# RMSNorm with SiLU on one core: VectorE's product moved ahead of the next block's sums in three blocks, and one more square given to VectorE in five

## Chip, cores, metric

One core of one Trainium2 chip, nothing else running on it. The metric is the device time of the kernel in microseconds (us), each figure the median of several runs. A profile of one execution goes with each kernel; its span is some 2 us shorter than the time, since a little of the time lies outside it.

## What is computed

The input x is 8 x 1024 rows of 2048 float32 values. Each row is divided by its root mean square, multiplied by gamma, and put through SiLU.

```python
def reference(x, gamma, eps):
    rms = np.sqrt(np.mean(x ** 2, axis=-1, keepdims=True) + eps)
    out = gamma * x / rms
    return (out * (1 / (1 + np.exp(-out)))).astype(np.float32)
```

## The kernel before

The rows are cut into 16 blocks of 4 MB: 128 partitions with four rows (J = 4) each. Six block buffers are kept (BUFS = 6). Loads are issued on ScalarE's queue, stores on SyncE's. In each block the sums of squares of two rows are taken by ScalarE and of two by VectorE; ScalarE takes the root, VectorE the inverse and the product with gamma, and ScalarE SiLU in place, on half a block at a time.

```python
    def sums(b, after_first=()):
        ss = small.tile([P, J], f32, name="ss")
        na = J // 2
        for j in range(na, J):
            nc.vector.tensor_tensor_reduce(out=junk_v, in0=row(b, j), in1=row(b, j), ...,
                                           accum_out=ss[:, j:j + 1])
        for j in range(na):
            nc.scalar.activation(out=junk_a, in_=row(b, j), func=ACT.Square,
                                 accum_out=ss[:, j:j + 1])
            if j == 0:
                for s in after_first:
                    load(s)
        ...                                   # root of the mean, on ScalarE

    def finish(b, halves=False):
        for j in range(J):
            nc.vector.scalar_tensor_tensor(out=row(b, j), in0=row(b, j), scalar=rstds[b][:, j:j + 1],
                                           in1=g, op0=ALU.mult, op1=ALU.mult)
            if j % 2:
                cols = slice((j - 1) * d, (j + 1) * d)
                nc.scalar.activation(out=blocks[b][:, cols], in_=blocks[b][:, cols], func=ACT.Silu)
                if halves:
                    nc.sync.dma_start(out=ob[b][:, cols], in_=blocks[b][:, cols])
    ...
        sums(0); invert(0); finish(0); store(0); sums(1); invert(1)     # six lines in the kernel
        for b in range(1, last - 1):
            sums(b + 1, after_first=[b + 3] if BUFS <= b + 3 < nblk else [])
            finish(b)
            store(b)
            invert(b + 1)
        finish(last - 1); store(last - 1)
        sums(last); invert(last); finish(last, halves=True)
```

## Time and profile before

| | before |
|---|---|
| time, median of 3 runs | 317.25 us (317.17 to 317.58) |
| span of the profile | 315.1 us |
| VectorE busy | 223.6 us, 71% |
| ScalarE busy | 223.7 us, 71% |
| bytes moved | 134.24 MB, mean 426 GB/s |
| DMA row of the slices | 9 in 38 of 40 slices |

How to read it: the page cuts the span into forty slices and gives the busy share of each in tenths (9 is 90% or more). DVE is VectorE, ACT is ScalarE, q10 the queue of the loads, q1 that of the stores. A busy share says how much an engine works, not whether the end waits for it: here two engines are at 71% and the sixteen DMA engines at 99%. The lines themselves stand in the prediction below.

### The profile page before, as it was taken

Reading aid. Unit: us, or ns where it says so; the run is one execution under the profiler, and the core shown is the slowest. Engines: PE = TensorE matmul, PEld = TensorE weight load, DVE = VectorE, ACT = ScalarE, POOL = GpSimd, SP = SyncE. Lnnn points to the kernel's source line nnn. Section 1 sums busy time; section 2 is a strip of 40 time slices with the busy share of each in tenths; the row PEclk is TensorE's granted clock in tenths of the full one; section 3 lists DMA queues with packets and bytes.
Section 4 is the critical chain, followed back from the end, with each engine's and each line's share of the span. In section 5 each row is a group of like instructions: output and inputs, shape, how many; then the busy total and the mean of one; then the engine's idle time right before and its main releaser. Section 6 shows DMA issues by size and latency. Waiting matters only on the chain.

```text
span 315.1 us, 438 instructions
## 1 busy us (share of the span) xinstructions
PE 2.1 (1%) x8; PEld 0.5 (0%) x8; DVE 223.6 (71%) x147; ACT 223.7 (71%) x144; POOL 0.2 (0%) x4
## 2 busy tenths in 40 slices
PE   0200000000000000000000000000000000000000
PEld 0000000000000000000000000000000000000000
DVE  0679499999295692957939488493984929994920
ACT  1357958999768677686676776766867668779550
POOL 0000000000000000000000000000000000000000
DMA  8999999999999999999999999999999999999997
GB/s 334 408 458 408 391 458 408 458 408 458 408 459 408 459 408 453 412 458 412 453 412 453 420 445 424 445 420 445 428 437 428 441 433 433 441 424 441 424 418 314
DMA packets 4762, 134.24 MB, mean 426 GB/s; under 512 B 532, under 2 KB 532, under 8 KB 536
## 3 DMA queue, kind: packets, MB, share of 16 engines
q10 hardware_dynamic: 2304, 67.11, 49.8%
q1 hardware_dynamic: 2456, 67.12, 49.4%
q14 instruction: 2, 0.02, 0.0%
HBM read 67.12 MB, written 67.11 MB: 426 GB/s over the span
## 4 chain that ended last, share of the span: by engine, by line
DMA 65%; DVE 18%; ACT 10%; issue 2%; DVEq 1%; ACTq 0%
DMA xt<-in_x_dram 65%; DVE xt L87 13%; ACT xt L91 6%; DVE junk_v L67 4%; ACT junk_a L71 2%; ACT L77 2%; DVEq L161 1%; ACT L91 0%; ACT rms L77 0%; DVE rstd L82 0%; DVE ss L67 0%; DVEq L67 0%; ACTq L77 0%
## 5 line engine op out<-in xcount | busy, mean ns | idle before, releaser
L87 DVE SCALAR_TENSOR_TENSOR xt<-xt,rstd,g 128x2048 f32<-128x2048 f32 x64 | 146.2, 2347 | 0.1
L91 ACT ACTIVATE xt<-xt 128x4096 f32<-128x4096 f32 x32 | 115.5, 3616 | 39.2 <-DVE xt L87 39.2
L67 DVE CUSTOM_DVE_ANT_0 junk_v<-xt 128x2048 f32<-128x2048 f32 x32 | 73.6, 2299 | 56.6 <-DMA xt<-in_x_dram 55.9
L71 ACT ACTIVATE junk_a<-xt 128x2048 f32<-128x2048 f32 x32 | 60.1, 1879 | 26.7 <-DMA xt<-in_x_dram 26.2
L77 ACT ACT_TABLE_LOAD x15 | 19.2, 1283 | 9.9 <-DVE ss L67 9.9
L91 ACT ACT_TABLE_LOAD x15 | 19.2, 1283 | 0.3
L82 DVE RECIPROCAL rstd<-rms 128x4 f32<-128x4 f32 x16 | 2.8, 173 | 10.8 <-ACT rms L77 10.8
L111 DVE COPY g<-junk_v 128x2048 f32<-128x2048 f32 x1 | 2.3, 2292 | 9.3 <-PE junk_v L109 9.3
L71 ACT ACTIVATION_READ_ACCUMULATOR junk_a<-xt 128x1 f32 x32 | 6.0, 186 | 0.0
L77 ACT ACTIVATE rms<-ss,eps_t 128x4 f32<-128x4 f32 x16 | 4.8, 297 | 1.3 <-DVE ss L67 1.1
L67 DVE DVE_READ_ACCUMULATOR2_ANT ss<- 128x1 f32 x32 | 4.5, 141 | 0.0
L104 ACT ACT_TABLE_LOAD x1 | 1.3, 1283 | 3.8 <-issue 3.8
L109 PE MATMUL junk_v<-grow,ones 1*128 1x512 f32 x8 | 2.1, 1132 | 8.1 <-DMA grow<-in_gamma_dram 8.1
L102 DVE MEMSET ones<- 128x128 f32 x1 | 0.2, 165 | 0.8 <-PEq L147 0.8
L109 PEld LDWEIGHTS junk_v<-grow,ones 1*128 1x128 f32 x8 | 0.5, 306 | 8.1 <-issue 8.1
L104 ACT ACTIVATE junk_a<-ones 128x1 f32<-128x1 f32 x1 | 0.2, 175 | 0.0
L147 POOL MEMSET const-bfloat16-1.0<- 128x1 bf16 x1 | 0.1, 101 | 0.0
L147 POOL MEMSET const-uint8-127<- 128x1 uint8 x1 | 0.1, 101 | 0.0
L147 POOL MEMSET const-float32-0.0<- 128x1 f32 x1 | 0.1, 98 | 0.2 <-issue 0.2
L147 POOL MEMSET const-float32-1.0<- 128x1 f32 x1 | 0.1, 98 | 0.0
L103 DVE MEMSET eps_t<- 128x1 f32 x1 | 0.1, 59 | 0.0
## 6 DMA issues: line engine op xcount, KB each, us to landing
xt<-in_x_dram ACTq DMA_DIRECT2D x16, 4096.0 KB, 38.7
out_dram<-xt SPq DMA_DIRECT2D x15, 4096.0 KB, 34.6
out_dram<-xt SPq DMA_DIRECT2D x2, 2048.0 KB, 9.0
grow<-in_gamma_dram SPq DMA_DIRECT2D x1, 8.0 KB
```

The source lines that it names most:

```text
L67: nc.vector.tensor_tensor_reduce(out=junk_v, in0=row(b, j), in1=row(b, j), scale=1.0, scalar=0.0, op0=ALU.mult, op1=ALU.add, accum_out=ss[ ...
L71: nc.scalar.activation(out=junk_a, in_=row(b, j), func=ACT.Square, accum_out=ss[:, j:j + 1])
L77: nc.scalar.activation(out=rms, in_=ss, func=ACT.Sqrt, scale=1.0 / d, bias=eps_t)
L82: nc.vector.reciprocal(out=rstd, in_=rmss.pop(b))
L87: nc.vector.scalar_tensor_tensor(out=row(b, j), in0=row(b, j), scalar=rstds[b][:, j:j + 1], in1=g, op0=ALU.mult, op1=ALU.mult)
L91: nc.scalar.activation(out=blocks[b][:, cols], in_=blocks[b][:, cols], func=ACT.Silu)
L102: nc.vector.memset(ones, 1.0)
L104: nc.scalar.activation(out=junk_a[:, 0:1], in_=ones[:, 0:1], func=ACT.Square)
L109: nc.tensor.matmul(junk_v[:, c * w:(c + 1) * w], ones[k:k + 1, :], grow[k:k + 1, :], start=True, stop=True)
L111: nc.vector.tensor_copy(out=g, in_=junk_v)
L147: nc = _bacc.Bacc("TRN2", target_bir_lowering=False, num_devices=1)
L161: with _tile.TileContext(nc) as tc:
```

## The change

Its intent: in the first three blocks the product, and with it the store, should not wait behind the next block's sums on VectorE; in the middle, ScalarE should be relieved of a square in every other block. The two functions `sums` and `finish` are split so that their parts can be put in any order. Cut to the core:

```diff
+    def share(b):
+        return 1 if 4 <= b <= 12 and b % 2 == 0 else 2      # rows whose squares ScalarE takes
...
-        for b in range(1, last - 1):
-            sums(b + 1, after_first=[b + 3] if BUFS <= b + 3 < nblk else [])
-            finish(b)
-            store(b)
-            invert(b + 1)
+        for b in range(last):
+            loads = [b + 3] if BUFS <= b + 3 < nblk else []
+            if b < SOON:                                    # SOON = 3
+                multiply(b)
+                squares_scalar(b + 1, loads)
+                silu(b)                                     # stores the block at its end
+                squares_vector(b + 1)
+                root(b + 1)
+            elif b < last - 1:
+                squares_scalar(b + 1, loads)
+                squares_vector(b + 1)
+                root(b + 1)
+                multiply(b)
+                silu(b)
+            else:
+                multiply(b)
+                silu(b)
+                ...                                         # squares and root of the last block
+            invert(b + 1)
```

More of the change, by code (lines that the diff above doesn't have):

```diff
@@ L50 @@
     junk_v = psum.tile([P, d], f32, name="junk_v")
-    blocks, rmss, rstds = {}, {}, {}
+    blocks, sss, rmss, rstds = {}, {}, {}, {}
     def load(b):
@@ L59, in row, with squares_scalar, squares_vector, root @@
         return blocks[b][:, j * d:(j + 1) * d]
-    def sums(b, after_first=()):
-        ss = small.tile([P, J], f32, name="ss")
-        na = J // 2
-        for j in range(na, J):
+    def squares_scalar(b, loads=()):
+        sss[b] = small.tile([P, J], f32, name="ss")
+        for j in range(share(b)):
+            nc.scalar.activation(out=junk_a, in_=row(b, j), func=ACT.Square,
+                                 accum_out=sss[b][:, j:j + 1])
+            if j == 0:
+                for s in loads:
+                    load(s)
+    def squares_vector(b):
+        for j in range(share(b), J):
             nc.vector.tensor_tensor_reduce(
                 out=junk_v, in0=row(b, j), in1=row(b, j), scale=1.0, scalar=0.0,
-                op0=ALU.mult, op1=ALU.add, accum_out=ss[:, j:j + 1])
-        for j in range(na):
-            nc.scalar.activation(out=junk_a, in_=row(b, j), func=ACT.Square,
-                                 accum_out=ss[:, j:j + 1])
-            if j == 0:
-                for s in after_first:
-                    load(s)
+                op0=ALU.mult, op1=ALU.add, accum_out=sss[b][:, j:j + 1])
+    def share(b):
+        return 1 if 4 <= b <= 12 and b % 2 == 0 else 2
+    def root(b):
         rms = small.tile([P, J], f32, name="rms")
-        nc.scalar.activation(out=rms, in_=ss, func=ACT.Sqrt, scale=1.0 / d, bias=eps_t)
+        nc.scalar.activation(out=rms, in_=sss.pop(b), func=ACT.Sqrt, scale=1.0 / d, bias=eps_t)
         rmss[b] = rms
@@ L83, in invert, with multiply @@
         rstds[b] = rstd
-    def finish(b, halves=False):
+    def multiply(b):
         for j in range(J):
@@ L88, in finish, with silu @@
                                            in1=g, op0=ALU.mult, op1=ALU.mult)
-            if j % 2:
-                cols = slice((j - 1) * d, (j + 1) * d)
-                nc.scalar.activation(out=blocks[b][:, cols], in_=blocks[b][:, cols], func=ACT.Silu)
-                if halves:
-                    nc.sync.dma_start(out=ob[b][:, cols], in_=blocks[b][:, cols])
+    def silu(b, halves=False):
+        for h in range(0, J, 2):
+            cols = slice(h * d, (h + 2) * d)
+            nc.scalar.activation(out=blocks[b][:, cols], in_=blocks[b][:, cols], func=ACT.Silu)
+            if halves:
+                nc.sync.dma_start(out=ob[b][:, cols], in_=blocks[b][:, cols])
+        if not halves:
+            store(b)
     def store(b):
@@ L114 @@
         last = nblk - 1
-        sums(0)
+        SOON = 3
+        squares_scalar(0)
+        squares_vector(0)
+        root(0)
         invert(0)
-        finish(0)
-        store(0)
-        sums(1)
-        invert(1)
-        for b in range(1, last - 1):
-            sums(b + 1, after_first=[b + 3] if BUFS <= b + 3 < nblk else [])
-            finish(b)
-            store(b)
-            invert(b + 1)
-        finish(last - 1)
-        store(last - 1)
-        sums(last)
-        invert(last)
-        finish(last, halves=True)
+        for b in range(last):
[15 more added lines that the diff above has]
+                silu(b)
+                squares_scalar(b + 1)
+                squares_vector(b + 1)
+                root(b + 1)
+            invert(b + 1)
+        multiply(last)
+        silu(last, halves=True)
 _INS = ['x', 'gamma', 'eps']
```

## The prediction

> **What bounds the kernel now.** I read the page's utilisation table and its slices first, because they say whether an engine, a wait or the transfers fill the span.
>
> ```profile
> span 315.1 us, 438 instructions
> PE 2.1 (1%) x8; PEld 0.5 (0%) x8; DVE 223.6 (71%) x147; ACT 223.7 (71%) x144; POOL 0.2 (0%) x4
> ...
> DMA  8999999999999999999999999999999999999997
> ...
> DMA packets 4762, 134.24 MB, mean 426 GB/s; under 512 B 532, under 2 KB 532, under 8 KB 536
> ...
> q10 hardware_dynamic: 2304, 67.11, 49.8%
> q1 hardware_dynamic: 2456, 67.12, 49.4%
> ```
>
> VectorE and ScalarE are both idle 29% of the span. The DMA row reads 9 in 38 of 40 slices, and loads (q10) and stores (q1) together take 49.8 + 49.4 = 99.2% of sixteen engines' time. The input is 67.11 MB and so is the output: each byte moves once in and once out, and no edit of the arithmetic alters that.
>
> Next the packet records of the trace. Each of the 16 DMA engines moves 67.11 x 2 / 16 = 8.39 MB, that is 256 packets of 32 KB. A packet takes 1.213 us (its median, and also its 95% range in the steady state), so one engine needs 256 x 1.213 = 310.5 us. The first packet starts at 2.07 us and the last ends at 314.2 us: 312.1 us in which, counted microsecond by microsecond, all 16 engines have a packet open. The 1.6 us between 310.5 and 312.1 are slow packets: 16 at the start (up to 2.3 us each) and some 27 between 34 and 38 us, when the first store joins the reads. So **the span is 2.1 us of start, 312.1 us of full transfer, 0.9 us of end**. The best schedule that I can imagine would win those 1.6 us, 0.5%.
>
> Then the list of waits, and the DMA issues of the same page.
>
> ```profile
> DVE junk_v L67 <- DMA xt<-in_x_dram: 55.9, 11, 5.5
> ACT xt L91 <- DVE xt L87: 39.2, 28, 3.6
> ACT junk_a L71 <- DMA xt<-in_x_dram: 26.2, 11, 7.9
> DVE rstd L82 <- ACT rms L77: 10.8, 3, 4.6
> ...
> xt<-in_x_dram ACTq DMA_DIRECT2D x16, 4096.0 KB, 38.7
> out_dram<-xt SPq DMA_DIRECT2D x15, 4096.0 KB, 34.6
> ```
>
> VectorE waits 55.9 us for loads: in eleven blocks the data comes late, not the engine. A 4 MB block lands 38.7 us after its load is issued, and its store 34.6 us after. A pair of one load and one store takes 19.37 us (loads are issued at 104.66, 124.02, 143.38 us). So each queue holds almost two blocks at any time: transfers wait for the transfer engines, these never wait for work. The chain that ended last says the same in its way, 65% of it a load of x. Its 13% of VectorE products and 10% of ScalarE are at the two ends, where I look below.
>
> **What the skill says, and whether the trace agrees.** "DMA: Bandwidth & Descriptors", section Specifications, gives a fabric ceiling of 435 GB/s and an HBM share of about 358 GB/s a core; "HBM Reference", section Specifications (TRN2), adds that one core streaming alone measures about 425. The trace has 426 over the span and 434 in the stretch from 66 to 259 us: the ceiling, with this core alone. The same DMA page, section Queues, rings and completion order, says that an engine takes turns between the queue rows that have work. That agrees with 16 open packets throughout, reads filling what stores leave. "ScalarE: Activation LUTs", section What ACT_TABLE_LOAD costs, gives 1283 ns for a table load; all 31 here take 1283.
>
> **The change, part by part.** From the grouped view by shape: a product (SCALAR_TENSOR_TENSOR) 2.347 us; a VectorE square 2.299 + 0.141 for its accumulator read, 2.44; a ScalarE square 1.88 + 0.19 = 2.07; a Silu of half a block 3.616; a root with its table load 1.28 + 0.30 = 1.58.
>
> (a) *Five middle blocks, 4, 6, 8, 10, 12.* One square each moves: VectorE gains 5 x 2.44 = 12.2 us (223.6 to about 236, 75%), ScalarE loses 5 x 2.07 = 10.3 us (to about 213, 68%). Per block VectorE then needs 4 x 2.347 + 3 x 2.44 + 0.17 = 16.9 us, in a period of 19.37 us: it still waits for loads, some 2.5 us instead of 5. What moves: the product of the block before starts 2.44 us later, and its store too. In the steady state the store of block b is issued some 12 to 14 us before the previous store has drained (block 4: issued 102.81, the one before drains at 116.9), so 2.44 us come out of a queue's depth. On the end of the span: 0.
>
> (b) *Blocks 0 to 2.* The product comes before the next block's sums on VectorE, and on ScalarE the next block's squares come before the Silu. I worked this through from measured landings (blocks 1, 2, 3 land at 23.1, 32.8, 49.3 us). Block 0: the product is at 19.87 to 29.02 as now; ScalarE squares block 1 from 23.2 to 27.3, loads its table to 28.6, two Silus to 35.9: store 0 is issued at 35.9, before 32.69, **3.2 us later**. Block 1: root at 37.5, product 37.7 to 46.8, second Silu to 50.5: store 1 at 50.5, before 55.77, **5.3 us earlier**. Block 2: product 52.4 to 61.5, store 2 at 65.2, before 69.74, **4.5 us earlier**. Then block 3: three squares of block 4 at 67.0 to 74.3, product to 83.5, store 3 at 87.2, before 83.72, 3.5 us later.
>
> The store queue now: store 0 issued at 32.69 has its first packet at 37.4; it drains at 55.0; store 1 starts at 59.6. So the reads have the engines alone for 35.3 + 4.6 = 39.9 us. After: to about 40.6, thus 38.5 us alone, and no hole after it because store 1 is there. In a shared period reads get half, so 1.4 us less alone means each later load lands about 1.4 us later. This is **a trade between reads and writes inside a full pipe**: not a microsecond of transfer time is saved or lost.
>
> (c) *What stays.* The last two blocks keep their order. Instructions, table loads and bytes are the same in number, the five moved squares aside.
>
> Where 1.4 us could matter is the tail: the last load lands at 279.2; the halves of the last block are issued at 300.39 and 304.91, and their first packets run at 303.7 and 308.6, when the transfers ahead have drained. Slack 3.3 and 3.7 us. With 1.4 us taken, 1.9 and 2.3 are left; an issue needs about 1.3 us to its first packet (0.73 to 2.07 at the start). It fits, narrowly. Sum: (a) 0, (b) 0 with a risk of up to 1 us, (c) 0: 317.25 plus nothing, **317.3 us**.
>
> **Rivals.**
> *One: VectorE was the bound, and earlier stores and a better split save time.* For it: the product's 13% of the last chain and the 10.8 us of waits for the root. Taken at face value, the three root waits of 4.6 us (blocks 1 and 2, and the last, which stays) would yield two times 4.6 = 9 us, giving 308. Against it: the transfers are full at that very time (33 to 56 us: DMA share 1.01), and 308 is below the 310.5 us that the packets alone need. It can't be.
> *Two: loads starve.* Load b+3 reuses the buffer of block b-3 and is issued on ScalarE's queue, so a late store would hold back both ScalarE and the reads. That would add several microseconds a block, 325 or more. Against: load 7 is wanted at about 87 us after the change, and store 1 lands at about 78; load 8 at about 106, store 2 at about 97. Margins of 9 us, more than 3.5.
> *Three: the tail is exposed.* If loads fall back by 3 us instead of 1.4, the two last half stores would leave holes of 1 to 1.5 us each: 318.5 to 320. My 1.4 rests on hand-made issue times, good to about 1 us.
> *Four: the slow packets go.* If the first store joins the reads more smoothly: 0.8 us less, 316.4. No reason to expect it, since the first store still joins a pipe of reads.
>
> **Range and chances.** The runs of before lie within 0.4 us. Below, rival four sets the edge, 316.5; above, a mild rival three, 318.4. Over 2% faster means under 311.0, which would need a transfer part of 305.9 us, under what the packets take: 1%, for a mistake of mine. Over 2% slower, over 323.7, needs rival two: 2%. Within 2%: 97%.
>
> **What would show it.** In the changed kernel's profile: bytes and the DMA row unchanged, 9 in slices 2 to 39; VectorE about 236 us and ScalarE about 213; VectorE's wait for loads down by some 12 us (each of five about 2.4 shorter); the first four stores issued near 35.9, 50.5, 65.2 and 87.2 us; the last half stores issued about 1.4 us later than now. I am wrong if a slice in the middle drops under 9, if the median packet isn't 1.213 us, or if a load waits for a store at its issue.

## The result

| | before | after |
|---|---|---|
| time, median of 6 runs | 317.33 us (317.13 to 317.69) | 316.97 us (316.88 to 317.27) |
| span of the profile | 315.1 us | 315.1 us |
| VectorE busy | 223.6 us | 235.8 us |
| ScalarE busy | 223.7 us | 213.4 us |

The ratio is 0.9989, with a 95% interval of 0.9976 to 1.0002: the same. Ratios here and below are the mean time of one kernel's fast runs over that of the other's of the same rounds, so they are not quite the ratios of the medians that are quoted. The 0.36 us between the medians lie inside that interval, and the two profiled spans agree to 0.03 us; no cause is given for them.

The page of the changed kernel, utilisation, slices and queues, as for the kernel before:

```profile
span 315.1 us, 436 instructions
...
PE 2.1 (1%) x8; PEld 0.5 (0%) x8; DVE 235.8 (75%) x157; ACT 213.4 (68%) x134; POOL 0.2 (0%) x4
...
DMA  8999999999999999999999999999999999999997
...
DMA packets 4763, 134.24 MB, mean 426 GB/s; under 512 B 533, under 2 KB 533, under 8 KB 537
...
q10 hardware_dynamic: 2304, 67.11, 49.7%
q1 hardware_dynamic: 2456, 67.12, 49.4%
...
DMA 68%; DVE 18%; ACT 8%; issue 1%; DVEq 1%; ACTq 0%
```

The last line is the chain of work that ended last, as shares of the span. The engines' busy times moved by 12.2 and 10.3 us; the DMA row is the same digit for digit. Next the list of waits and the DMA issues of the changed kernel (in a wait: total us, how often, the longest; in an issue: count, size, us to landing):

```profile
DVE junk_v L74 <- DMA xt<-in_x_dram: 41.6, 11, 5.9
ACT xt L99 <- DVE xt L93: 33.5, 27, 3.6
ACT L83 <- DVE ss L74: 27.4, 12, 5.3
ACT junk_a L66 <- DMA xt<-in_x_dram: 20.5, 7, 7.8
DVE rstd L88 <- ACT rms L83: 12.9, 5, 4.6
...
xt<-in_x_dram ACTq DMA_DIRECT2D x16, 4096.0 KB, 38.7
out_dram<-xt SPq DMA_DIRECT2D x15, 4096.0 KB, 29.8
```

Where did 12 us of VectorE work go? VectorE's wait for loads fell from 55.9 to 41.6 us: the work went into waiting time. ScalarE's 10.3 us became a wait of its own: its wait for VectorE's sums (the table load before the root) grew from 9.9 to 27.4 us, while its waits for loads and for products fell by 5.7 us each. VectorE's wait for the root did not shrink: 12.9 us in five waits, after 10.8 in three. The stores now take 29.8 instead of 34.6 us from issue to landing, in the median. The engines' slack has moved about; a load still lands 38.7 us after its issue.

The timeline of the store issues, before (start us, us, queue, line, operation): blocks 0 to 3, then the two halves of the last block.

```profile
32.69 0.36 SPq L96 DMA_DIRECT2D out_dram<-xt  x1
55.77 0.33 SPq L96 DMA_DIRECT2D out_dram<-xt  x1
69.74 0.33 SPq L96 DMA_DIRECT2D out_dram<-xt  x1
83.72 0.33 SPq L96 DMA_DIRECT2D out_dram<-xt  x1
...
300.39 0.33 SPq L93 DMA_DIRECT2D out_dram<-xt  x1
304.91 0.33 SPq L93 DMA_DIRECT2D out_dram<-xt  x1
```

And of the changed kernel:

```profile
35.19 0.35 SPq L106 DMA_DIRECT2D out_dram<-xt  x1
49.84 0.33 SPq L106 DMA_DIRECT2D out_dram<-xt  x1
65.55 0.33 SPq L106 DMA_DIRECT2D out_dram<-xt  x1
88.17 0.33 SPq L106 DMA_DIRECT2D out_dram<-xt  x1
...
300.55 0.33 SPq L101 DMA_DIRECT2D out_dram<-xt  x1
305.07 0.33 SPq L101 DMA_DIRECT2D out_dram<-xt  x1
```

Store 1 goes out 5.9 us earlier and store 2 4.2 us earlier, as intended; stores 0 and 3 go out 2.5 and 4.5 us later. At the end 0.16 us of later issue is all that can be seen of it. The packet records show why. Store 1, issued 5.9 us earlier, lands only 1.3 us earlier (77.6 us for 78.9): what was issued earlier stood in a queue longer. Counting each open packet by the part of it that is past, the old kernel has moved 24.5 MB at 60 us and the new one 24.6.

### The profile page after: what moved, and what is told of

It reads as the page before. It is cut to its first block, busy times and chain, and to the rows that moved or that the text cites. A ratio compares the mean times of both kernels' runs of the same rounds, so it can differ in the third digit from the quotient of the medians.

```text
span 315.1 us, 436 instructions
## 1 busy us (share of the span) xinstructions
PE 2.1 (1%) x8; PEld 0.5 (0%) x8; DVE 235.8 (75%) x157; ACT 213.4 (68%) x134; POOL 0.2 (0%) x4
## 4 chain that ended last, share of the span: by engine, by line
DMA 68%; DVE 18%; ACT 8%; issue 1%; DVEq 1%; ACTq 0%
DMA xt<-in_x_dram 68%; DVE xt L93 14%; DVE junk_v L74 4%; ACT xt L99 4%; ACT junk_a L66 2%; ACT L83 1%; DVEq L184 1%; ACT L99 0%; ACT rms L83 0%; DVE rstd L88 0%; DVE ss L74 0%; ACTq L55 0%; ACTq L83 0%; DVEq L74 0%
## 5 line engine op out<-in xcount | busy, mean ns | idle before, releaser
L74 DVE CUSTOM_DVE_ANT_0 junk_v<-xt 128x2048 f32<-128x2048 f32 x37 | 85.1, 2300 | 42.3 <-DMA xt<-in_x_dram 41.6
L66 ACT ACTIVATE junk_a<-xt 128x2048 f32<-128x2048 f32 x27 | 50.6, 1875 | 20.8 <-DMA xt<-in_x_dram 20.5
L83 ACT ACT_TABLE_LOAD x15 | 19.2, 1283 | 27.5 <-DVE ss L74 27.4
L88 DVE RECIPROCAL rstd<-rms 128x4 f32<-128x4 f32 x16 | 2.8, 173 | 12.9 <-ACT rms L83 12.9
L74 DVE DVE_READ_ACCUMULATOR2_ANT ss<- 128x1 f32 x37 | 5.2, 141 | 0.0
L66 ACT ACTIVATION_READ_ACCUMULATOR junk_a<-xt 128x1 f32 x27 | 5.0, 186 | 0.0
## 6 DMA issues: line engine op xcount, KB each, us to landing
xt<-in_x_dram ACTq DMA_DIRECT2D x16, 4096.0 KB, 38.7
out_dram<-xt SPq DMA_DIRECT2D x15, 4096.0 KB, 29.8
```

The costliest lines, as they stand in the source:

```text
L83: nc.scalar.activation(out=rms, in_=sss.pop(b), func=ACT.Sqrt, scale=1.0 / d, bias=eps_t)
L88: nc.vector.reciprocal(out=rstd, in_=rmss.pop(b))
```

## The experiments

Theory T is the prediction's: the transfer engines are full and the bytes set the time. Rival R: the engines' chain sets it, and a gain in the first blocks and a loss in the middle cancel. All experiments start from the changed kernel. Where a difference to the changed kernel is given, it is that of the medians, 316.97 us being the changed kernel's.

### Each half of the change alone

Only the new order, with two squares everywhere:

```diff
-        return 1 if 4 <= b <= 12 and b % 2 == 0 else 2
+        return 2
```

> The new order of blocks 0 to 2 alone, two squares on each engine everywhere. Theory T (the transfer engines are full, only bytes count): ratio to the kernel before 0.997 to 1.001, stores 0 to 2 issued within 0.5 us of the changed kernel's 35.2, 49.8, 65.6. Rival R (the engines' chain sets the time; a gain in the first blocks and a loss in the middle cancel): clearly faster than the kernel before, by 4 us or more (ratio under 0.99), two root waits of 4.6 us having gone.

Measured: 317.46 us (before in the same rounds 317.40), ratio 1.0002, interval 0.9989 to 1.0014. Stores 0 to 2 were issued at 35.28, 49.92 and 65.64 us.

Only the five moved squares, with the old order:

```diff
-        SOON = 3
+        SOON = 0
-            elif b < last - 1:
+            elif 0 < b < last - 1:
```

(and the loads passed on in the last branch, which block 0 now takes, too).

> The five moved squares alone, the old order of the first blocks. Theory T: ratio to the kernel before 0.997 to 1.002, VectorE busy 235.8 us. Rival R: slower than the kernel before by 4 to 12 us (ratio over 1.012), because VectorE carries 12.2 us more.

Measured: 317.08 us, ratio 0.9994, interval 0.9981 to 1.0006; VectorE busy 235.4 us. Neither half does anything that can be measured, to within intervals of 0.13%, or 0.4 us. So nothing larger cancels, and rival R's second half falls.

### Take away VectorE's squares

```diff
-                out=junk_v, in0=row(b, j), in1=row(b, j), scale=1.0, scalar=0.0,
+                out=junk_v[:, 0:64], in0=row(b, j)[:, 0:64], in1=row(b, j)[:, 0:64], scale=1.0, scalar=0.0,
```

> The changed kernel with VectorE's squares cut to 64 of 2048 columns: wrong result on purpose, the same bytes. VectorE busy falls by some 75 us, to about 160. Theory T: 316.5 to 317.5 us, no faster than the changed kernel. Rival R (VectorE's share of the chain, 18% of the span, is time to be won): 300 us or less, and at least 7 us from the first and the last blocks.

Measured: 317.16 us, ratio to before 0.9997, interval 0.9982 to 1.0013; the result is wrong, as meant. From this kernel's page and its list of waits:

```profile
PE 2.1 (1%) x8; PEld 0.5 (0%) x8; DVE 159.4 (51%) x157; ACT 213.3 (68%) x134; POOL 0.2 (0%) x4
...
DMA  8999999999999999999999999999999999999997
...
DVE junk_v L74 <- DMA xt<-in_x_dram: 95.7, 12, 10.1
```

VectorE lost 76.4 us of work, a third of what it had, and its wait for loads grew by 54 us. The last two half stores were issued 4.1 us earlier than in the changed kernel (296.41 us for 300.55), and the end did not move. The 18% of the chain that ended last which the page gives to VectorE was no time to be won.

### Fewer bytes, and more bytes

Half of block 8 is not read, and VectorE fills the other half with a copy:

```diff
-        nc.scalar.dma_start(out=xt, in_=xb[b])
+        if b == 8:
+            nc.scalar.dma_start(out=xt[:, 0:2 * d], in_=xb[b][:, 0:2 * d])
+        else:
+            nc.scalar.dma_start(out=xt, in_=xb[b])
     def squares_vector(b):
+        if b == 8:
+            nc.vector.tensor_copy(out=blocks[b][:, 2 * d:], in_=blocks[b][:, 0:2 * d])
```

> The changed kernel with only half of block 8 read (2 MB less) and the other half filled by a VectorE copy from the first: wrong result on purpose, fewer bytes and more work on VectorE (one copy, 2 to 4.5 us). Theory T: faster by 64 packets x 2 x 1.213 us / 16 x 0.5 = 4.85 us, thus about 312.1 us. Rival R: same or slower by up to 4 us.

Measured: 312.41 us, ratio 0.9845, interval 0.9831 to 0.9858: 4.6 us less than the changed kernel, with 2.2 us more on VectorE (238.0). The result is wrong.

Block 8 stored twice:

```diff
             store(b)
+            if b == 8:
+                store(b)
```

> The changed kernel with block 8 stored twice (the same values, so a right result; 4 MB more, no arithmetic more). Theory T: slower by 128 packets x 1.213 us / 16 = 9.7 us, about 326.7 us. Rival R: the store queue has room in the span, so up to 2 us slower.

Measured: 328.00 us (four runs, 326.69 to 328.10), ratio 1.0322, interval 1.0303 to 1.0342. That is 11.0 us more than the changed kernel, where 9.7 were expected; only the lowest run meets the expected number. In the profiled run, which took 327.96 us, the packets took 10.3 us more on each engine: 9.7 us for the bytes and 0.55 us of packets over 1.213 us. The DMA engines' last packets also ended less evenly. Why most runs have this last microsecond and one has not is open. The edit also did more than add bytes: the second store of block 8 was issued only at 214.64 us, when the first had landed (214.63). Store 9 went out at 215.08 us instead of 202.25, and load 14, which reuses block 8's buffer, at 237.02 instead of 221.02. So no store packet ran from 213 to 218 us and no load packet from 235 to 241, and each time the other queue filled the engines: the DMA row is at 9 throughout.

Both experiments agree with T in sign and within 1.3 us in size; R has no place for either.

### How much VectorE can be loaded

All four squares of blocks 4 to 13 on VectorE:

```diff
-        return 1 if 4 <= b <= 12 and b % 2 == 0 else 2
+        return 0 if 4 <= b <= 13 else 2
         sss[b] = small.tile([P, J], f32, name="ss")
+        if share(b) == 0:
+            for s in loads:
+                load(s)
```

> The changed kernel with all four squares of blocks 4 to 13 on VectorE: 4 x 2.347 + 4 x 2.44 + 0.2 = 19.3 us a block, just under the 19.37 us of a load and a store. VectorE busy about 272 us (86%). Theory T: still 316.5 to 318 us. Rival R: slower by 15 of the moved squares x 2.44, some 37 us at most, and by 5 us at least.

Measured: 317.73 us, ratio 1.0017, interval 1.0004 to 1.0031. VectorE at 86%, its wait for loads down to 6.2 us in nine waits, and the time 0.8 us over that of the changed kernel.

One square more per block, on top of that edit:

```diff
+    def extra(b, n):
+        for _ in range(n):
+            nc.vector.tensor_tensor_reduce(out=junk_v, in0=row(b, 0), in1=row(b, 0), ..., accum_out=junk_s)
...
                 root(b + 1)
+                extra(b + 1, 1 if 4 <= b + 1 <= 13 else 0)
                 multiply(b)
```

> As the one before with one more square a block on VectorE in blocks 4 to 13: 21.8 us a block, now over the period of 19.37 us. Theory T says that the bound changes hands here: VectorE runs without a pause from about 67 us, reaches the squares of block 14 some 24 us late, and the time is 335 to 341 us. If the bound were anything else than the larger of transfers and VectorE a block, it would differ from this by more than 5 us.

Measured: 332.10 us, ratio 1.0464, interval 1.0450 to 1.0478. The page:

```profile
DVE  0679697979999999999999999999999999999460
...
DMA  8999999999999999999999999999999997859958
```

VectorE is at 9 from slice 10 to slice 37, and for the first time the DMA row has holes. The bound has changed hands, as T said. The size is 3 us below the lower end expected. The timeline shows the mis-sized term, at the first squares of two blocks:

```profile
89.36 2.27 DVE L78 CUSTOM_DVE_ANT_0 junk_v<-xt 128x2048 f32<-128x2048 f32 x1
...
110.26 2.27 DVE L78 CUSTOM_DVE_ANT_0 junk_v<-xt 128x2048 f32<-128x2048 f32 x1
```

From one to the other it is 20.90 us, not the 21.8 that the durations add up to. VectorE's instructions start before the one in front has ended: four products of 2.347 us take 9.14 us together, and squares of 2.30 + 0.14 us follow each other every 2.39 us. So the excess over the 19.37 us of a load and a store is 1.53 us a block, 15.3 us in ten blocks, and the time rose by 15.1.

### The end of the kernel

Squares added on VectorE between the last block's inverse and its product, one in the first run and three in the second, with the same `extra`:

```diff
+        extra(last, 1)      # 3 in the second run
         multiply(last)
```

> The changed kernel with one square more (2.44 us) on VectorE between the last block's inverse and its product. Theory T: the last half stores are issued at about 303.0 and 307.5 us, the transfers ahead of them drain at 303.7 and 308.6, an issue needs about 1.3 us: a hole of 0 to 1 us, time 317 to 318. Rival R (the last block's chain on the engines sets the end): the whole 2.44 us, 319.4.

> The changed kernel with three squares more (7.3 us) at the same place. Theory T: about 2 us of it are covered by transfers still draining, so 4.8 to 6 us slower: 322 to 323. Rival R: the whole 7.3 us, 324.3. A third view (the store queue is so deep that the tail is hidden): under 320.

Measured: with one, 317.21 us, ratio 0.9995 (0.9982 to 1.0007). With three, 321.96 us, ratio 1.0146 (1.0131 to 1.0161), 5.0 us over the changed kernel. Three squares at 2.39 us are 7.2 us; 2.2 of them were covered. The slices of the run with three:

```profile
DMA  8999999999999999999999999999999999999947
...
GB/s 329 435 418 455 398 394 459 435 418 459 394 460 435 419 451 406 451 435 422 455 406 451 426 426 455 406 451 426 426 455 414 443 431 422 451 418 443 394 197 328
```

The 4 and the 197 GB/s in slice 39 are the hole: the store of block 14 had drained by 304.1 us, the half store was issued at 307.52, and its first packet ran at 308.35. So the tail has about two microseconds of slack, after which it is exposed one to one. The third view (a tail hidden deeply) falls.

### What keeps the transfer engines full

```diff
-    BUFS = 6
+    BUFS = 5        # 4 in the second run
```

> The changed kernel with five block buffers instead of six: load b+3 then waits, on ScalarE's queue, for store b-2 instead of b-3. Theory T: as long as both queues hold work the time stays within 1%; ScalarE will stand behind the load in some blocks. The prediction's second rival (loads starve, each costing several microseconds a block) would show here if anywhere: over 325 us, and a DMA row with digits under 9 in the middle.

Measured: 316.92 us, ratio 0.9985, interval 0.9969 to 1.0002. The list of waits and the issues of this kernel:

```profile
ACT junk_a L66 <- DMA out_dram<-xt: 40.1, 6, 7.4
...
ACT L83 <- DMA out_dram<-xt: 22.0, 4, 5.5
...
xt<-in_x_dram ACTq DMA_DIRECT2D x16, 4096.0 KB, 25.9
out_dram<-xt SPq DMA_DIRECT2D x15, 4096.0 KB, 26.2
```

ScalarE now stands behind its load instructions, which wait for stores, for 62.1 us in ten waits, and both queues are shorter; its DMA row stays at 9. Here even a waiting ScalarE cost nothing: a transfer lands some 26 us after its issue and a pair takes 19.37, so each queue still holds more than one block.

> Four block buffers: load b+3 waits for store b-1, which has only just been issued. Now the loads must starve: at least a store's drain (9.7 us alone) of each block is seen by ScalarE. Expected over 340 us, DMA row with many digits under 9. If even this stays at 317, the depth of the queues is not what keeps the transfer engines full.

Measured: 366.80 us, ratio 1.1560, interval 1.1543 to 1.1578. The page, and two of its waits:

```profile
DMA  8999989979799778997889978899788997796988
...
ACT junk_a L66 <- DMA out_dram<-xt: 76.7, 7, 14.2
...
ACT L83 <- DMA out_dram<-xt: 38.9, 4, 9.7
```

A load now lands 12.2 us after its issue and a store 12.0 us: the queues hold about one transfer each, and the DMA row has 7s and 8s. This is the prediction's second rival, brought about on purpose. It is real, but one has to take away two buffers of six to meet it.

## Why the prediction was right

The time, 316.97 us for 317.3, lies in the range. Point by point:

- **The full pipe** held. The median packet is again 1.213 us, the bytes and the DMA row are unchanged, and time follows bytes: 4.6 us less for 2 MB less, 11.0 more for 4 MB more (the second 1.3 us above its estimate).
- **Part (a)** held. VectorE went to 235.8 us and ScalarE to 213.4, for 236 and 213 predicted. VectorE's wait for loads fell by 14.3 us, for 12 predicted; new waits came on ScalarE, which the prediction didn't name and which cost nothing.
- **Part (b)**: the four store issues came at 35.19, 49.84, 65.55 and 88.17 us, each within a microsecond of those worked out by hand. **The trade between reads and writes** shows in the packets. Each transfer ends in sixteen packets of 4 bytes, which I take to be one from each DMA engine. By their means stores 4 and 8 end 1.1 us earlier (135.28 us for 136.41, and 212.74 for 213.87), and loads 5, 14 and 15 end 0.8 to 0.9 us later (load 14: 258.74 for 257.89). The two experiments with half the change agree: load 14 has its mean at 257.93 us in the old order (only_share) and at 258.82 in the new (only_order).
- What failed in part (b) is the step "each later load lands about 1.4 us later", and with it "the last half stores issued about 1.4 us later". The squares of block 14, which start on its landing, first before and then after:

```profile
259.66 2.30 DVE L67 CUSTOM_DVE_ANT_0 junk_v<-xt 128x2048 f32<-128x2048 f32 x1 [5.54 <-DMA xt<-in_x_dram]
...
259.81 2.30 DVE L74 CUSTOM_DVE_ANT_0 junk_v<-xt 128x2048 f32<-128x2048 f32 x1 [5.51 <-DMA xt<-in_x_dram]
```

The last halves are issued 0.16 us later, not 1.4. Two terms were wrong.

The first is the time in which the reads have the DMA engines alone, 39.9 us before and 38.5 after in the prediction. The first store packets of the sixteen engines start at 37.33 us on average before and at 39.60 after. Stores 0 and 1 end 22.76 us apart before and 19.36 after, for a usual 19.4, so the old hole was 3.4 us, not 4.6, and the new order has none, as predicted. The reads thus have 39.60 - 37.33 = 2.3 us more at the start and lose the hole of 3.4: 1.1 us less, not 1.4. (In only_order the same sum gives 0.9, and load 14 is 0.9 later there.)

The second term was left out: a load has landed when the last of its sixteen closing packets has ended. For load 14 the first and the last of these lay 1.8 us apart before and 0.9 after, and the last ended at 259.18 and 259.34 us. This spread differs from profile to profile (2.2 us in only_share, 1.5 in only_order, 2.0 in the run with one square more at the end, 0.8 in that with three), so the 0.16 us is no more than the profiles differ by. What sets the spread was not looked into.

- **The tail** is as narrow as was said: one square more there is free within the interval, three cost 5.0 us. With its real lag of 0.16 us the change used next to nothing of that slack, and a lag of 1.4 us would have fitted too, since the run with one square more issued its halves 2.7 us later. So the forecast of the time did not hang on the step that failed.
- **Rival one** (308 us) is refuted by the run without VectorE's squares: a third of its work gone, and no gain. **Rival two** (starving loads) needs four buffers. The margins were as predicted: load 7 was issued at 84.91 us, and store 1's last packet had ended at 77.3; load 8 at 104.61, store 2's at 96.9. **Rival three** (an exposed tail) appears only with added work, and **rival four** (the slow packets go) in part at most: slow packets cost 1.22 us an engine instead of 1.48 in the two profiles, which is less than the runs differ by.
- **The prediction's clock for packets** was 0.33 us late against that of the instructions: it has 2.07 us for the first packet and 314.2 for the end of the last, where the records, counted from the page's first instruction, have 1.74 and 313.87. Its landing times are late by the same amount. Block 14 of the kernel before tells which zero is right: it landed at 259.52 us and its first square on ScalarE started at 259.55, while by the prediction's zero it would have landed after that, at 259.85. Differences between packet times stay; the slack of the last halves is 3.0 and 3.4 us instead of 3.3 and 3.7, and the 1.3 us from an issue to its first packet are 1.0, so what is left is the same.
- **VectorE's need per block**, 16.9 us by the sum of durations, was too high for the same reason as in the run over the period: the instructions overlap a little. It changed nothing here.

## What to carry to other kernels

Before reordering engines, count the packets: here packets per engine times the packet's duration filled 310.5 of 315.1 us, and what was left to gain was fewer bytes and the two ends, whatever share of the "last chain" the compute engines held. What could be spent freely in this kernel is also worth knowing: one block buffer, and VectorE work up to four products and four squares a block. That is some 18.5 us (an estimate, 20.90 less one square's 2.39) and took 0.8 us over the changed kernel; at 20.90 us, over the 19.37 us of a load and a store, VectorE set the time. Count such work by the distance from one instruction's start to the next and not by the sum of durations. Check the tail apart, since there even a full pipe had only two microseconds to give.

## What the Trainium skill lacked or had wrong

- "DMA: Bandwidth & Descriptors", section Where 436 GB/s comes from, says that for transfers between HBM and SBUF the HBM side binds, at about 358 GB/s, though it adds that its own measurement of 16 MB was 425. Here 426 GB/s over the span and 434 in the middle were measured on one core with reads and writes mixed; "HBM Reference", section Specifications (TRN2), has this right for a core alone.
- The same DMA page, section Specifications, gives about 0.6 us to the first byte on this path. It does not say from which instant. From the start of the issue instruction to the first packet it took 0.83 us with both queues empty (the first half store with three squares more, 307.52 to 308.35), 1.01 us at the kernel's start, and 4.2 to 4.4 us for the first store that joined a queue of reads (35.19 to 39.43 after, 32.69 to 37.09 before). I found no page with this last figure; its mechanism was not tested.
- "Perfetto Trace Analysis", section Optimizing Scalar/DVE Operations, says that part of a profiled instruction's latency overlaps with the next instruction. The runs agree, and it is worth a number that the page hasn't: a VectorE block of 21.8 us by the sum of durations took 20.90 us. I had not used it, and the expectation of the run over the period was 3 us or more too high for it.
- I found no page that says how much queue depth a mixed stream of loads and stores needs: here five 4 MB buffers did as well as six (ratio to before 0.9985), and four cost 15.6%.
